# Decoder block on one core: first two units interleaved, silu and sigmoid by tanh, units and selectors in another order, last norm in three steps

## The chip, the cores and the metric

The kernel runs on 1 core of one Trainium2 chip. The metric is the device time of one execution in microseconds (us). The engines are called as in the profile: PE (matmuls; PEld is its weight loading), ACT (activations, casts and copies), DVE (elementwise work on two operands), POOL (here only DMA issues that accumulate, and memsets) and SP (DMA issues). L188 is line 188 of the kernel before.

## The reference

One decoder block on x (512 tokens, 1024 channels), with 16 learned meta tokens ahead of it. All is in float32.

```python
xn = rmsnorm(h, norm1_g)
(mq, mk, mv, mi, mf, mo, gq, gk, gv, ga, gr, gate_m, gate_g) = split(xn @ w_in)
mq, mk = silu(causal_conv(concat(mq, mk)))            # 4 taps per channel
logi, logf = mi + b_i, log_sigmoid(mf + b_f)
hm = mlstm(mq, mk, mv, logi, logf)                    # 4 heads, exp gates, running max
y_m = head_rmsnorm(hm) * sigmoid(mo)
loga = log_sigmoid(ga @ g_a2 + b) / 16
y_g = head_rmsnorm(gla(gq, gk, gv, loga)) * silu(gr)  # 4 heads
h = h + (sigmoid(gate_m) * (y_m @ w_branch_m) + sigmoid(gate_g) * (y_g @ w_branch_g)) @ w_out
h = h + (silu(hn @ w_ff_gate) * (hn @ w_ff_up)) @ w_ff_down     # hn = rmsnorm(h, norm2_g)
out = rmsnorm(h, final_g)                             # meta tokens dropped
```

## The kernel before, in words

Everything is kept transposed, channels on the partitions and tokens along the row: 528 tokens (16 meta, 512 real). Precision is kept by parts: a float32 operand is split into a high part (`hi`, a cast on ACT) and a low part (`lo`, the rest, a subtraction on DVE), and a product is three matmuls, hi*hi, hi*lo and lo*hi (`mm3`, L302 to L304).

The work of PE is a list of units (`job_list`, L51). A unit is 128 output channels against all 1024 inputs; its weights are one 128x1024 tile, loaded by SP (`load_raw`, L181), cast by ACT (`whi`, L188) and subtracted by DVE (`wlo`, L193), some units ahead (`begin`). A unit over all 528 tokens is 8 x 2 x 3 matmuls of 264 columns in two PSUM banks (`unit_all`), one over the 512 real tokens 8 x 3 of 512 in one bank (`unit_real`). From the unit gm0 on, many units go in pairs (`pair`, L350 on): seven products of half size in place of eight (L344 to L346), whose sums are put together by ACT copies (L404, L405, L407) and DVE rows.

The order of the units is: gates, then for each mLSTM head h mq, mk, two mv, two mo; then the pairs gm (gates of the branch) with the GLA units gq/gk, gv, gr; then bm, gg, bg, out, and the feed-forward fg, fu, down. The order of all instructions on each engine is written by the program itself: side work (conv, gate rows, mLSTM heads, normalised x) is held in generators, and after each step of a unit `tick` lets each of them issue a little; the numbers after `yield` are ticks to stand by. All engines run their queue in order. There are eight PSUM banks, used in turn (`bank`), so a matmul that starts a bank waits for whoever reads that bank's earlier contents.

The start: SP loads parameters, the first weights and x, eight tiles x0 to x7. ACT and DVE split weights and x times norm1_g (L471), ACT squares x, DVE adds the squares up (L482). PE runs the unit gates, then the unit mq0, both on x that is not yet divided by its norm, and then the matmul with ones (L1078), which sums the squares over channels. `rsqrt_mean` (L489) makes rstd of it: Ln and Exp on ACT and one Newton step on DVE (L496 to L500). Later evacuations multiply by rstd (L593, L615), until `normed_x` (L508, L517) has made divided x.

For the mLSTM, `conv` (L707, L716) puts four taps on ACT and DVE, `conv_act` applies silu on ACT and splits q and k (L730, L732). `gate_rows` (L633 on) makes the log gates, cumulated along the tokens, on 32 partitions; PE transposes their copies (L699) into one bank, which DVE copies to `acol` (L693). Each head (`mlstm`, L868) needs `acol`, casts its selector `sel` on ACT (L872), waits six ticks, spreads gate rows over partitions by two matmuls (L875, L876) in two banks, reads them (L879 copy on ACT, L880 on DVE, `em` by Exp on ACT), and then multiplies exps with q-k products (L897 to L899, L904) and values (L939 to L941).

[...] `act` (L130 to L132) gives the function its set: Exp and Ln one set, Silu one, Sigmoid one; a row ACT_TABLE_LOAD stands where the set changes.

At the end `final` (L1482 to L1495) makes the last norm for the second half of the tokens: Ln and Exp on ACT, four rows on DVE (L1488 to L1491), four products with the output tiles and their DMAs.

## Time and profile before

| | |
|---|---|
| three timed runs, median | 948.4 us |
| three timed runs, lowest and highest | 947.27 and 948.83 us |
| the profiled execution, its own time | 948.52 us |
| its span, first to last instruction | 946.7 us |
| mean granted clock of TensorE | 0.992 |
| PE busy, first and last matmul | 917.5 us, 6.56 and 937.5 us |
| DVE, ACT busy | 636.2, 546.2 us |
| ACT_TABLE_LOAD | 35 rows of 1.28 us |

A row of a timeline gives the start, the length, the engine, line and operation, the tiles written and read, their shapes, a count, and in brackets how long the engine idled before it and which engine, tile and line released it. A row of a window gives for PE, PEld, DVE, ACT and POOL the busy time and the number of instructions, and then the granted clock, the DMA share and GB/s. Matmuls overlap: two that follow each other start closer than either is long.

### The profile page before, as it was taken

The numbers are of one execution on the slowest core, as the hardware profiler recorded it, in microseconds if no ns is written. First come the engines' busy times: TensorE is split into PE (matmuls) and PEld (weight loads), VectorE is DVE, ScalarE is ACT, GpSimd is POOL, SyncE is SP. The second block draws the span as 40 slices with busy tenths as digits, with TensorE's granted clock in tenths as the row PEclk, the third lists the DMA queues.
The fourth block names the chain that finished last, engine by engine and source line by source line (L and its number), as shares of the span: only waits on it lengthen the run. The fifth ranks groups of instructions, "written<-read, shape, count | busy, mean of one in ns | idle before, by whom it ended". The sixth has DMA issues, their size and how long they took to land.

```text
span 946.7 us, 15478 instructions
## 1 busy us (share of the span) xinstructions
PE 917.5 (97%) x6083; PEld 842.3 (89%) x6083; DVE 636.2 (67%) x940; ACT 546.2 (58%) x954; POOL 86.8 (9%) x102
## 2 busy tenths in 40 slices
PE   6999999989999999999999999999999999999995
PEld 6988899878998899999998888888999999888885
DVE  6797776767875577777777556785767767842323
ACT  7557788779684256766874334443555555732321
POOL 0000022001100011110100000212121110000000
PEclk9999999989999999999999999999999999999998
DMA  7245375345562466655643343335788885322302
GB/s 262 101 139 155 119 162 123 75 112 134 127 163 90 111 148 155 163 120 141 134 134 107 116 133 116 107 102 132 185 186 179 189 191 148 115 94 85 111 1 89
DMA packets 48712, 124.45 MB, mean 131 GB/s; under 512 B 5376, under 2 KB 11520, under 8 KB 48640
## 3 DMA queue, kind: packets, MB, share of 16 engines
q1 hardware_dynamic: 35008, 101.32, 34.5%
q0 software_dynamic: 12544, 21.11, 14.5%
q8 instruction: 47, 0.77, 0.3%
q10 hardware_dynamic: 1088, 1.05, 0.3%
q14 instruction: 25, 0.20, 0.1%
HBM read 118.08 MB, written 5.37 MB: 130 GB/s over the span
## 4 chain that ended last, share of the span: by engine, by line
PE 78%; ACT 9%; DVE 8%; issue 3%; DMA 1%; DVEq 0%; SPq 0%; ACTq 0%
PE b L303 13%; PE b L302 13%; PE b L304 13%; PE b L344 12%; PE b L345 11%; PE b L346 11%; ACT t L132 4%; ACT whi L188 2%; DVE wlo L193 1%; ACT L130 1%; PE b L1056 1%; DVE t L716 1%; PE b L1058 1%; PE b L1035 1%; ACT L132 1%
## 5 line engine op out<-in xcount | busy, mean ns | idle before, releaser
L303 PE MATMUL b<-t,whi 128*128 128x512 f32 (+2 forms) x822 | 289.9, 353 | 1.0 <-DVE t L471 0.7
L302 PE MATMUL b<-t,whi 128*128 128x512 f32 (+2 forms) x774 | 274.0, 354 | 6.7 <-ACT t L132 6.6
L304 PE MATMUL b<-t,wlo 128*128 128x512 f32 (+2 forms) x774 | 270.8, 350 | 0.0
L344 PE MATMUL b<-t,whi 128*128 128x256 f32 (+1 forms) x864 | 250.0, 289 | 7.7 <-ACT t L404 6.1
L346 PE MATMUL b<-t,wlo 128*128 128x256 f32 (+1 forms) x864 | 245.1, 284 | 0.0
L345 PE MATMUL b<-t,whi 128*128 128x256 f32 (+1 forms) x864 | 245.0, 284 | 0.0
L193 DVE TENSOR_TENSOR wlo<-raw,whi 128x1024 fp32r<-128x1024 f32 x155 | 193.1, 1249 | 50.8 <-ACT whi L188 50.5
L188 ACT CAST whi<-raw 128x1024 fp32r<-128x1024 f32 x155 | 161.7, 1047 | 64.5 <-PE b L345 27.4
L303 PEld LDWEIGHTS b<-t,whi 128*128 128x128 f32 x822 | 155.8, 190 | 23.3 <-DVE t L843 1.1
L344 PEld LDWEIGHTS b<-t,whi 128*128 128x128 f32 x864 | 164.3, 190 | 9.9 <-ACT t L404 7.2
L302 PEld LDWEIGHTS b<-t,whi 128*128 128x128 f32 x774 | 147.0, 190 | 26.5 <-ACT t L132 6.6
L345 PEld LDWEIGHTS b<-t,whi 128*128 128x128 f32 x864 | 164.3, 190 | 0.5
L304 PEld LDWEIGHTS b<-t,wlo 128*128 128x128 f32 x774 | 146.8, 190 | 19.9 <-DVE wlo L193 0.3
L346 PEld LDWEIGHTS b<-t,wlo 128*128 128x128 f32 x864 | 164.0, 190 | 0.0
L132 ACT ACTIVATE t<-t 128x512 f32<-128x512 f32 (+6 forms) x124 | 70.4, 588 | 29.8 <-DVE t L1289 9.3
L183 POOL DMA_DIRECT2D raw<-wst x36 | 31.2, 867 | 364.4 <-DMA wf<-wst 104.9
L188 ACT CAST whi<-wf 128x1024 fp32r<-128x1024 f32 x36 | 37.8, 1051 | 22.5 <-PE b L345 13.5
L132 ACT ACTIVATE t<-f 128x256 f32<-128x256 f32 (+1 forms) x24 | 11.6, 482 | 61.6 <-DVE f L1456 61.6
L212 POOL DMA_DIRECT2D wf<-wst x36 | 32.5, 912 | 155.3 <-DMA wf<-wst 85.7
L193 DVE TENSOR_TENSOR wlo<-wf,whi 128x1024 fp32r<-128x1024 f32 x36 | 43.9, 1218 | 0.0
L1456 DVE TENSOR_TENSOR f<-f,b 128x512 f32<-128x512 f32 (+1 forms) x9 | 5.7, 629 | 53.3 <-PE b L304 53.3
L344 PE MATMUL b<-t,wgh 128*128 128x256 f32 (+1 forms) x144 | 41.0, 285 | 0.0
(219 smaller groups left out, 1216.6 us busy)
## 6 DMA issues: line engine op xcount, KB each, us to landing
raw<-wst SPq DMA_DIRECT2D x155, 512.0 KB, 3.6
wf<-wst SPq DMA_DIRECT2D x36, 256.0 KB, 3.2
wf<-wst POOLq DMA_DIRECT2D x36, 256.0 KB, 5.4
raw<-wst POOLq DMA_DIRECT2D x36, 256.0 KB, 4.7
t<-xT SPq DMA_DIRECT2D x8, 264.0 KB, 5.6
pos<-t SPq DMA_DIRECT2D x8, 264.0 KB, 2.3
t<-xT SPq DMA_DIRECT2D x8, 256.0 KB, 3.8
t<-neg POOLq DMA_DIRECT2D x6, 272.0 KB, 6.3
```

The costliest lines, as they stand in the source:

```text
L130: S.preload_act_table_set(want)
L132: S.activation(o, i, func, **kw)
L183: G.dma_start(lr(r, 0), lr(wst[v - 1], 0), accum_op=ALU.add)
L188: S.copy(t, src)
L193: V.tensor_tensor(t, src, hi.bitcast(F32), ALU.subtract)
L212: G.dma_start(lr(st.f, 1), lr(wst[u + 1], 1), accum_op=ALU.add)
L302: T.matmul(o, w_h, ah[:, c0:c1], start=first, stop=False)
L303: T.matmul(o, w_h, al[:, c0:c1], start=False, stop=False)
L304: T.matmul(o, w_l, ah[:, c0:c1], start=False, stop=last)
L344: T.matmul(o, h, xh_[k][:, c0:c1], start=start and k == 0, stop=False, skip_group_check=not start)
L345: T.matmul(o, h, xl_[k][:, c0:c1], start=False, stop=False, skip_group_check=not start)
L346: T.matmul(o, l, xh_[k][:, c0:c1], start=False, stop=k == 3, skip_group_check=not start)
```

## The change

- **First two units side by side.** `first_units` runs gates and mq0 together, for each of the eight parts of x first the six matmuls of the one, then the six of the other. Their weights are loaded, cast and subtracted in halves, between the loads and splits of x0 to x4. Ten matmuls of a constant tile with itself are issued ahead of them. The additions of the squares have one weight subtraction (unit 2) among them.
- **Tables.** Sigmoid becomes tanh of half the argument, with the plus one put into the product that follows (`branch`, the head's output) and the half into a later factor (`halfg`, the split of the branch sum). Silu of q and k becomes tanh, one more DVE row (L778 of the changed kernel) and a half in the split (L783, L786). Exp and tanh are asked from one set, `exp_and_others`; Exp keeps the set that is there if it has it. Silu of gr and of the feed-forward stays.
- **Order of the units.** The two mo of a head come after mq and mk of the next.
- **Gate rows.** The unit gates is copied from its banks by ACT right after the first units, and multiplied by rstd in one DVE row.
- **Selectors.** The first is cast at the end of `gate_rows`' row part, each next one right after the two matmuls of the head before; the six ticks go.
- **Weights** are split one unit less far ahead of time up to the fifth unit, and from there in a later place of the unit (`LATE`) until the distance is made up.
- **Last norm.** (sum + n eps)(-0.5/n) is made from the bank beside Ln and Exp, and the Newton step after them has two rows and the final product in one: three in place of four. The last output DMA goes out on SP, not on ACT.

```diff
-TABLE = {AF.Exp: LOGEXP, AF.Ln: LOGEXP, AF.Silu: "silu", AF.Sigmoid: "sigmoid"}
+TABLE = {AF.Exp: (LOGEXP, TANHEXP), AF.Ln: (LOGEXP,), AF.Tanh: (TANHEXP,), AF.Silu: ("silu",)}
...
-        o += one(("mq", h), ("mk", h), ("mv", 2 * h), ("mv", 2 * h + 1), ("mo", 2 * h), ("mo", 2 * h + 1))
+        o += one(("mq", h), ("mk", h)) + (mo(h - 1) if h else []) + one(("mv", 2 * h), ("mv", 2 * h + 1))
+    o += mo(H - 1)
...
-        if want is not None and want != table[0]:
-            if want == LOGEXP:
-                S.preload_act_table_set(want)
-            table[0] = want
+        if want is not None and table[0] not in want:
+            table[0] = want[0]
+            if func != AF.Silu:
+                S.preload_act_table_set(want[0])
...
+    LATE = {"s": [(split_hi, 4), (split_lo, 6)]}
...
         if all(i[0] == "s" for i in ITEMS[n - 2:n + 1]) and len(names) == 1 and more:
             n += 1
+            if u > 4 and ready[0] < min(n, len(ITEMS)) - 1:
+                tables = [PLAIN, LATE]
...
+    for _ in range(10):
+        T.matmul(idle[:, :P], ones, ones, start=True, stop=True)
...
-        gsb = tt()
-        for a in range(2):
-            c = slice(a * HALF, (a + 1) * HALF)
-            V.tensor_tensor(gsb[:96, c], ps[0][a][:96], rstd[:96, c], ALU.mult)
+        V.tensor_tensor(gsb[:96], gsb[:96], rstd[:96], ALU.mult)
...
         for b, a in ((q, src[0].v), (k, src[1].v)):
-            act(a, a, AF.Silu)
+            t = tt(n=a.shape[1])
+            act(t, a, AF.Tanh, scale=0.5)
+            V.scalar_tensor_tensor(a, t, 1.0, a, ALU.add, ALU.mult)
...
-            S.copy(hi, a)
+            act(hi, a, AF.Copy, scale=0.5)
             yield 2
-            V.tensor_tensor(lo, a, hi.bitcast(F32), ALU.subtract)
+            V.scalar_tensor_tensor(lo, a, 0.5, hi.bitcast(F32), ALU.mult, ALU.subtract)
...
+    def selector(h):
+        gts.sel = mpool.tile([P, 2, P], F32R, tag="sel", name=nm("sel"), bufs=1)
+        S.copy(gts.sel, cn[:, NS + h:NS + 8:H].unsqueeze(2).to_broadcast([P, 2, P]))
...
-    ps_g = unit_all(("gates", 0))
-    ps_q = unit_all(("mq", 0))[0]
+        for k in range(KT):
+            for o, ws in zip(ps, w):
+                for a in range(2):
+                    mm3(o[a], ws, k, X.h[k], X.l[k], a * HALF, (a + 1) * HALF, k == 0, k == KT - 1)
...
-        V.tensor_tensor(t, ps, t, ALU.mult)
+        V.scalar_tensor_tensor(t, t, 1.0, ps, ALU.add, ALU.mult)
...
         act(y, ps, AF.Ln, bias=b_eps, scale=1.0 / D)
+        V.tensor_scalar(x, ps, D * EPS, -0.5 / D, op0=ALU.add, op1=ALU.mult)
         act(y, y, AF.Exp, scale=-0.5)
         yield 1
         V.tensor_tensor(t, y, y, ALU.mult)
-        V.scalar_tensor_tensor(t, ps, D * EPS, t, ALU.add, ALU.mult)
-        V.tensor_scalar(t, t, -0.5 / D, 1.5, op0=ALU.mult, op1=ALU.add)
-        V.tensor_tensor(y, y, t, ALU.mult)
+        V.tensor_tensor(t, t, x, ALU.mult)
+        V.scalar_tensor_tensor(y, t, 1.5, y, ALU.add, ALU.mult)
```

Three places of the order that the program writes. The first is DVE's queue around the copy of the gate columns (`acol`). Before, the copy stands behind the first conv row (L716) of head 1's q:

```order
L508 SCALAR_TENSOR_TENSOR t_137_767<-t_5_79,pr_69,t_64_317 128x528
L707 MEMSET t_138_769 128x3
L593 TENSOR_TENSOR t_138_769<-b_122_669,t_64_317 128x264
L593 TENSOR_TENSOR t_138_769<-b_123_670,t_64_317 128x264
L716 SCALAR_TENSOR_TENSOR t_139_779<-t_138_769,pr_69,t_139_779 128x512
L693 COPY acol_574<-b_132_714 128x480
```

The same place in the changed program, where L767 is the conv row, L778 the plus one of tanh, L786 the low part of q or k, L561 and L570 rows of the normalised x, and L197 a low part of weights:

```order
L767 SCALAR_TENSOR_TENSOR t_134_770<-t_133_763,pr_71,t_134_770 128x528 x3
L197 TENSOR_TENSOR wlo_140_799<-raw_101_581,whi_135_776 128x1024
L570 TENSOR_TENSOR t_137_779<-t_132_761,t_136_778 128x528
L778 SCALAR_TENSOR_TENSOR t_122_698<-t_141_817,t_122_698 128x512
L778 SCALAR_TENSOR_TENSOR t_134_770<-t_142_821,t_134_770 128x528
L561 SCALAR_TENSOR_TENSOR t_147_837<-t_6_83,pr_71,t_64_335 128x528
L786 SCALAR_TENSOR_TENSOR t_144_829<-t_122_698,t_143_828 128x512
L744 COPY acol_604<-b_139_789 128x480
L786 SCALAR_TENSOR_TENSOR t_149_844<-t_134_770,t_148_843 128x528
```

The copy (L744) now has the convs of head 1's q and k, their tanh rows and the split of q ahead of it.

The second is PE's queue. Before, the spread of the gate rows for head 0 (L875, L876) stands inside the unit mv2 (banks 152 and 153):

```order
L304 MATMUL b_153_850<-t_15_122,wlo_121_657 128x264
L875 MATMUL b_157_866<-t_96_545,sel_144_799 128x512
L876 MATMUL b_158_867<-t_96_545,sel_144_799 128x512
L302 MATMUL b_152_849<-t_17_126,whi_115_638 128x264
L303 MATMUL b_152_849<-t_18_128,whi_115_638 128x264
```

In the changed program it is in the unit mo1, 22 rows before mv2 begins (banks 171 and 172); these rows are that beginning:

```order
L820 MATMUL b_170_911<-pr_71,t_92_505 128x128
L820 MATMUL b_170_911<-pr_71,t_102_590 128x128
L309 MATMUL b_171_916<-t_16_134,whi_123_707 128x264
L310 MATMUL b_171_916<-t_19_140,whi_123_707 128x264
L311 MATMUL b_171_916<-t_16_134,wlo_129_734 128x264
L309 MATMUL b_172_917<-t_16_134,whi_123_707 128x264
```

By the turn of the banks, 171 is the bank of the gate columns (139, read by `acol`'s copy), 172 the one of em (155).

The third is ACT's queue ahead of the first copy of the pair gm0 (L404 before), which also holds the sigmoid of mo6 and mo7 (L132 out of a bank) and the rows of head 3:

```order
L132 ACT_TABLE_LOAD
L132 ACTIVATE t_2302<-b_2122 128x512
L132 ACTIVATE t_2303<-b_2206 128x512
L879 COPY t_2329<-b_2319 128x512
L188 CAST whi_2338<-raw_2123 128x1024
L130 ACT_TABLE_LOAD
L132 ACTIVATE t_2331<-b_2320,cb 128x512
L404 COPY t_2293<-b_2289 128x256
```

In the changed program the copy is L411, tanh stands for sigmoid, and L973 is a cast of head 3's weights `wh`:

```order
L135 ACT_TABLE_LOAD
L136 ACTIVATE t_444_2420<-b_400_2232 128x512
L136 ACTIVATE t_445_2421<-b_422_2324 128x512
L973 CAST wh_394_2198<-t_431_2377 128x16
L990 CAST t_448_2446<-t_397_2204 128x512
L192 CAST whi_450_2452<-raw_401_2233 128x1024
L411 COPY t_442_2411<-b_438_2407 128x256
```

The load between the sigmoids and em is gone from here, and head 3's work stands further along at this point.

## The prediction

> **What bounds the kernel now.** I read the page first, then the waits of PE by stretch, then the windows, then the timelines of single places. The page says that PE is the engine that counts:

> ```profile
> span 946.7 us, 15478 instructions
> PE 917.5 (97%) x6083; PEld 842.3 (89%) x6083; DVE 636.2 (67%) x940; ACT 546.2 (58%) x954; POOL 86.8 (9%) x102
> ```

> The profiled execution took 948.52 us, 1.8 more than its span and 0.1 more than the median of 948.4. With PE at 97%, the change can gain only what PE waits, what it runs at a lower clock, and the ends. The waits of PE from 71.2 to 280 us, and before that:

> ```profile
> PE b L344 <- ACT t L404: 5.6, 3, 3.6
> PE b L939 <- DVE t L757: 1.6, 1, 1.6
> PE b L344 <- ACT t L405: 1.1, 1, 1.1
> PE b L748 <- ACT t L591: 0.5, 1, 0.5
> PE b L302 <- DVE t L757: 0.2, 1, 0.2
> ...
> PE b L875 <- ACT sel L872: 1.9, 1, 1.9
> ```

> The columns are total, times and longest. The five rows of 71 to 280 us sum to 9.0 us, and 3.6 of it is one wait. It has a second price, which the windows show:

> ```profile
> 195.73 0.39 PE L899 MATMUL b<-t,t 128*128 128x512 f32 x1
> 199.71 0.58 PE L344 MATMUL b<-t,whi 128*128 128x256 f32 x1 [3.59 <-ACT t L404]
> ...
> 198.40:205.20 6.80, 5.49 (x24) 0.50 0.62 152
> ```

> In a window row the length, PE's busy time and then the granted clock stand: 0.50 for 6.8 us. PE worked from 199.71 to 205.2, 5.5 us, at half speed: 2.7 us lost at most; against the spacing of the same matmuls elsewhere I find 2.3, and take 2.5. The wait at 67.44 was shorter, and left the clock alone:

> ```profile
> 67.44 0.28 PE L304 MATMUL b<-t,wlo 128*128 128x264 f32 x1
> 69.60 0.50 PE L875 MATMUL b<-t,sel 128*128 128x512 f32 x1 [1.87 <-ACT sel L872]
> ...
> 60.00:80.00 20.00, 18.00 (x139) 17.24 (x138) 18.48 (x30) 14.01 (x25) 0.00 (x0) 1.00 0.54 178
> ```

> So a wait of 2 us costs itself, one of 3.6 costs about 6. The window also shows DVE (its third pair) busy for 18.48 of 20 us just there: in this stretch DVE has nothing to spare, though its mean over the span is 67%.

> **The change part by part.** *First units.* The sum of squares (L1078) starts as soon as PE has ended two units:

> ```profile
> 22.23 1.06 PE L1078 MATMUL b<-t,ones 128*128 128x264 f32 x4
> ...
> 13.67 1.44 DVE L471 SCALAR_TENSOR_TENSOR t<-t,pr,t 128x528 fp32r<-128x528 f32 x2
> 15.02 5.59 DVE L482 TENSOR_TENSOR t<-t,t 128x528 f32<-128x528 f32 x7
> 20.53 3.49 DVE L193 TENSOR_TENSOR wlo<-raw,whi 128x1024 fp32r<-128x1024 f32 x3
> 24.52 0.71 DVE L496 TENSOR_TENSOR t<-t 128x528 f32<-128x528 f32 x1 [0.50 <-ACT t L132]
> ```

> DVE's sum was ready at 20.6, PE came at 22.23. Now PE can start on half a tile of weights instead of a whole one, which I put at 2 us earlier for all of its 96 matmuls, 20.2, and more if the ten dummy matmuls bring the clock up early. Then DVE's sum is last, or as late: seven additions 5.59 plus one subtraction now placed among them (3.49/3, 1.2) is 6.8, and they start at 13.4 to 14.0, for x arrives as before (the halves move the same bytes on the same queue). That gives 20.2 to 20.8; I take 20.3, 1.9 earlier. An idle PE of 1 to 2 us ahead of it should leave the clock, by the wait at 67.44; the bound is 2.5 lost. L496 came 2.29 after the start of L1078, so its successor (L549) starts at 22.6.

> *DVE between there and the gate columns.* The new order of units puts mq1 and mk1 ahead of mo0 and mo1, and the tanh form of silu puts one more row on DVE for each q and k. All this is ahead of the copy of the gate columns (acol), which now follows both convs. Durations of what comes in addition:

> ```profile
> L193 DVE TENSOR_TENSOR wlo<-raw,whi 128x1024 fp32r<-128x1024 f32 x6 | 7.3, 1209 | 0.0
> L593 DVE TENSOR_TENSOR t<-b,t 128x264 f32<-128x264 f32 x10 | 3.8, 423 | 0.1
> L716 DVE SCALAR_TENSOR_TENSOR t<-t,pr,t 128x512 f32<-128x512 f32 x5 | 3.7, 749 | 1.2 <-ACT t L132 1.1
> L615 DVE TENSOR_TENSOR t<-b,t 128x512 f32<-128x512 f32 x2 | 1.3, 670 | 0.0
> L732 DVE TENSOR_TENSOR t<-t,t 128x512 fp32r<-128x512 f32 x1 | 0.7, 691 | 0.0
> ...
> 43.36 0.70 DVE L649 TENSOR_TENSOR t<-t,t 32x528 f32<-32x528 f32 x1 [3.13 <-ACT t L132]
> ...
> 68.15 0.65 DVE L693 COPY acol<-b 128x480 f32<-128x480 f32 x1
> 68.72 1.53 DVE L716 SCALAR_TENSOR_TENSOR t<-t,pr,t 128x512 f32<-128x512 f32 x2
> ```

> Counted in the order of both programs, from L496 to acol: one subtraction more (1.2), five rows of conv more (3.8), the four new tanh rows, which have L716's form (3.0), a third split of q and k, all three in the dearer form (0.9), two evacuations more (0.8); two L615 fewer (-1.3), one gate row for two (-0.1). That is 8.3; rows overlap by up to 0.08 (acol ends at 68.80, the next starts at 68.72), so I take 7.7. Before, the way from 24.52 to 68.80 took 44.3, waits included (3.13 of them for Ln at 43.36). I keep the waits: the new tanh rows wait for ACT too, but ACT drops two table loads there, and the sign is open, +-3. acol then ends at 22.6 + 44.3 + 7.7 = 74.6, against 68.8.

> *Who waits for that.* In the changed program mv2's first matmul takes the PSUM bank that acol's copy empties, its second bank that of the exponentials em on ACT. ACT reaches em from the second split of k, which waits for the tanh row of DVE that ends 2.1 ahead of acol. From there it has seven rows:

> ```profile
> L188 ACT CAST whi<-raw 128x1024 fp32r<-128x1024 f32 x155 | 161.7, 1047 | 64.5 <-PE b L345 27.4
> L132 ACT ACTIVATE t<-t 128x512 f32<-128x512 f32 (+6 forms) x124 | 70.4, 588 | 29.8 <-DVE t L1289 9.3
> ```

> one cast of weights (1.05) and six of the size of the second row or half of it (3.1): 4.1, less 2.1, so em is 2.0 behind acol, at 76.6. PE itself, by before's 71.1 for the same amount of matmuls, less the wait of 2.0 and the 1.9 gained, would be there at 67.2, or 71 where lower parts of mk1 and mo0 come late; both waits lie under the later one. So PE goes on at 76.6: 5.5 behind before's row:

> ```profile
> 71.15 0.29 PE L304 MATMUL b<-t,wlo 128*128 128x264 f32 x1
> ```

> Its last wait, 5 to 6 us, is longer than the 3.59 that halved the clock, so 2.5 more; nothing to 3.4 as bounds.

> *Later waits, and ACT.* One set now serves tanh and exp, and the changed program holds 26 table loads where the one before holds 35, these 34 and one first:

> ```profile
> L130 ACT ACT_TABLE_LOAD x17 | 21.8, 1283 | 0.3
> L132 ACT ACT_TABLE_LOAD x17 | 21.8, 1283 | 0.3
> ...
> 193.59 1.28 ACT L132 ACT_TABLE_LOAD   x1
> 194.89 1.09 ACT L132 ACTIVATE t<-b 128x512 f32<-128x512 f32 x2
> 197.41 1.28 ACT L130 ACT_TABLE_LOAD   x1
> 199.29 0.36 ACT L404 COPY t<-b 128x256 f32<-128x256 f32 x1
> ...
> 179.37 0.65 ACT L591 COPY t<-b 128x264 f32<-128x264 f32 x2
> ```

> By the rows that is 9 x 1.28 = 11.5 us of ACT, and none of PE unless ACT is what PE waits for. [...] From 77 to gm0 DVE and ACT have room, as a window of that stretch shows (third and fourth pair):

> ```profile
> 120.00:140.00 20.00, 20.00 (x132) 18.20 (x130) 15.36 (x29) 16.25 (x34) 4.86 (x4) 1.00 0.73 162
> ```

> The selector is cast a head earlier, and the waits at L939, L748 and L302 should go. At gm0 the wait need not: the product q6 adds into the bank of q1, and waits for ACT's copy s1 of it (L404), which stood 20.3 us behind the evacuation at 179.37. In the new order the same two ends hold 43 rows with still two loads (2.6) and four casts of weights (4.2); by the durations of the same forms in this trace they sum to 20.5. The exps of the last head have come in where two waits were. So I let the 3.6 and its 2.5 of clock stand, as they stood. Of the other 5.4 of waits I let 0.5 stand: gain 4.9, with 0 as the other bound, since half of them lie behind gm0, where ACT is fullest.

> *Small ones.* Branch products turn from TENSOR_TENSOR to the STT form, +0.06 each, off the path while PE is ahead. The last output goes out on SP instead of ACT: I take that as nothing, with the length of the row below as the bound either way. In the tail one row leaves the chain:

> ```profile
> 939.84 0.29 DVE L1490 TENSOR_SCALAR t<-t 128x256 f32<-128x256 f32 x1
> ```

> It goes beside Ln, -0.3.

> **The sum** against the profiled 948.52: +5.5 (mv2) +2.5 (clock there) -4.9 (later waits) -0.3 (tail) = +2.8, 951.3. The gain of 1.9 at the start is inside the 5.5.

> **Rivals.** *1. ACT is in time at gm0* and the clock stays full: PE's lag from mv2 has let ACT run ahead, or the rows of the last head are done before 179. It decides once 3.6 of ACT's 20.5 us are done earlier. For it speaks that by the program 11 loads stand ahead of that copy where 18 stood, 9 us less; against it that the two inside stay. -3.6 -2.5: 945.2, faster.

> *2. DVE is earlier at acol.* The Ln wait of 3.13 goes, since silu's load no longer stands before it. acol at 71.5, PE resumes at 73.5, the wait at mv2 is under 3 us and the clock stays: -3.1 -2.5, 945.7, faster.

> *3. The waits in the gate stage stay*, with ACT as late as its window of 220 to 240 shows it (the fourth pair):

> ```profile
> 220.00:240.00 20.00, 18.93 (x144) 18.58 (x145) 13.78 (x25) 19.01 (x36) 3.06 (x5) 1.00 0.53 130
> ```

> +4.9: 956.2, slower by more than the forecast.

> [...]

> **How the numbers follow.** A measurement here can tell 0.2%, 1.9 us, from no change: same is 946.5 to 950.3. The forecast has 0.45, with its own range of 948.3 to 954.3 from the +-3 of DVE's waits: 0.32 of it above 950.3, 0.11 same, 0.02 below. Rival 1 has 0.20 (0.16 faster, 0.04 same), rival 2 0.18 (0.13 and 0.05), rival 3 0.17, slower. Together: faster 0.31, same 0.20, slower 0.49. The range of 944.5 to 956.0 takes in both faster rivals singly and half of the third; both faster ones at once (939) and the far end of the third are left out.

> **What would show it.** Right: L1164 (the sum of squares) near 20.3; acol's copy near 74; mv2's first matmul behind a wait of 4 us or more and a half clock near 77 to 83; at gm0 a wait of 3 to 4 for the copy s1 (L411). Wrong: PE at mv2 before 73 with no halving, or no wait at gm0. Also wrong, with a result near 948, if the time comes out by the start and tail alone.

## The result and the profile after

The changed kernel takes 957.3 us in the median of four runs (956.93 to 957.45), the kernel before 948.0 in the same comparison. The ratio is 1.0098 with a 95% interval of 1.0085 to 1.0111: slower by 9.3 us. The forecast was slower by 2.8, at 951.3, with 956.0 as the end of its range. The way was right, the size was not. Executions that were disturbed are left out of all comparisons, and since the only profile of the run e12 is of such an execution (1288 us), nothing is read from it.

The head of the page and the five largest of the waits of PE over the whole span (total, times, longest):

```profile
span 955.4 us, 15518 instructions
PE 923.8 (97%) x6103; PEld 847.0 (89%) x6103; DVE 643.5 (67%) x950; ACT 538.1 (56%) x948; POOL 86.7 (9%) x102
...
PE b L351 <- ACT t L411: 8.2, 3, 6.0
PE b L309 <- DVE acol L744: 3.9, 1, 3.9
PE b L1164 <- DVE t L533: 2.4, 1, 2.4
PE b L311 <- DVE wlo L197: 2.1, 2, 1.5
PE b L309 <- ACT t L136: 1.5, 2, 0.9
```

ACT has lost 8 us of work. PE waits more than before in three places: 8.2 for the copies of the pairs (L411, before 6.1), 3.9 for acol, 2.4 for the sum of squares. The timeline of PE, and of DVE at acol:

```profile
20.98 2.01 PE L1164 MATMUL b<-t,ones 128*128 128x264 f32 x4 [2.40 <-DVE t L533]
...
24.22 0.71 DVE L549 TENSOR_TENSOR t<-t 128x528 f32<-128x528 f32 x1 [2.16 <-ACT t L136]
...
75.80 0.65 DVE L744 COPY acol<-b 128x480 f32<-128x480 f32 x1
...
76.59 0.56 PE L309 MATMUL b<-t,whi 128*128 128x264 f32 x1 [3.87 <-DVE acol L744]
78.49 0.59 PE L309 MATMUL b<-t,whi 128*128 128x264 f32 x1 [0.90 <-ACT t L136]
...
204.75 0.28 PE L353 MATMUL b<-t,wlo 128*128 128x256 f32 x1
211.03 0.58 PE L351 MATMUL b<-t,whi 128*128 128x256 f32 x1 [6.00 <-ACT t L411]
```

The first of the two waits at mv2 is for acol's bank, the second for em's, as forecast. The wait at gm0 is 6.0, not 3.6. Three windows of the granted clock (length, PE busy, then the clock):

```profile
21.20:24.50 3.30, 3.30 (x12) 2.89 (x12) 1.14 (x2) 2.10 (x4) 0.00 (x0) 0.50 0.66 248
75.80:82.50 6.70, 5.01 (x20) 4.72 (x21) 5.88 (x11) 6.54 (x16) 0.00 (x0) 0.50 0.44 144
208.90:215.60 6.70, 4.57 (x21) 4.57 (x22) 3.24 (x7) 3.00 (x6) 1.72 (x2) 0.50 0.73 122
```

Between the start and the last matmuls the clock was halved three times, each time behind a wait; in the kernel before, once.

To see where the 8.7 us of the span went I compared the times at which both kernels reach the same amount of matmul work, each matmul weighed with its usual spacing. This distance is called the lag from here on, and its place is given by the time in the profile of before. By that the changed kernel is 3.8 us ahead at the end of the first two units, 0.5 behind at 30 us, 4.5 behind from 55 to 67 (parts of weights that come late, L192 and L197), 9.4 at 72 to 100, 7.1 at 104, 6.9 at 195, 9.2 at 210 behind gm0, 6.5 at 222, 7.8 at 250, and 8.7 at the end.

### The profile page after: what moved, and what is told of

Its sections match the earlier page's. It is cut to its first block, busy times and chain, and to the rows that moved or that the text cites. A ratio compares the mean times of both kernels' runs of the same rounds, so it can differ in the third digit from the quotient of the medians.

```text
span 955.4 us, 15518 instructions
## 1 busy us (share of the span) xinstructions
PE 923.8 (97%) x6103; PEld 847.0 (89%) x6103; DVE 643.5 (67%) x950; ACT 538.1 (56%) x948; POOL 86.7 (9%) x102
## 3 DMA queue, kind: packets, MB, share of 16 engines
q10 hardware_dynamic: 1232, 1.09, 0.3%
## 4 chain that ended last, share of the span: by engine, by line
PE 85%; DVE 7%; ACT 5%; issue 2%; DMA 1%; SPq 0%; DVEq 0%; ACTq 0%
PE b L309 14%; PE b L310 14%; PE b L311 14%; PE b L351 12%; PE b L353 12%; PE b L352 12%; ACT t L136 3%; DVE wlo L197 1%; PE b L1123 1%; ACT L135 1%; DVE t L767 1%; PE b L1125 1%; PE b L1102 1%; ACT whi L192 1%; DMA t<-xT 1%
## 5 line engine op out<-in xcount | busy, mean ns | idle before, releaser
L197 DVE TENSOR_TENSOR wlo<-raw,whi 128x1024 fp32r<-128x1024 f32 x153 | 191.1, 1249 | 82.4 <-ACT whi L192 82.1
L192 ACT CAST whi<-raw 128x1024 fp32r<-128x1024 f32 x153 | 160.0, 1046 | 97.6 <-PE b L310 52.3
L136 ACT ACTIVATE t<-t 128x512 f32<-128x512 f32 (+6 forms) x139 | 80.0, 593 | 51.0 <-DVE t L1171 26.7
L192 ACT CAST whi<-wf 128x1024 fp32r<-128x1024 f32 x36 | 37.8, 1050 | 23.5 <-PE b L352 13.8
L197 DVE TENSOR_TENSOR wlo<-wf,whi 128x1024 fp32r<-128x1024 f32 x36 | 43.8, 1217 | 0.0
L351 PE MATMUL b<-t,wgh 128*128 128x256 f32 (+1 forms) x144 | 40.9, 284 | 0.0
L352 PE MATMUL b<-t,wgh 128*128 128x256 f32 (+1 forms) x144 | 40.8, 284 | 0.0
L353 PE MATMUL b<-t,wgl 128*128 128x256 f32 (+1 forms) x144 | 40.8, 283 | 0.0
```

The lines of the kernel that those rows point to most:

```text
L136: S.activation(o, i, func, **kw)
L192: S.copy(t, src)
L197: V.tensor_tensor(t, src, hi.bitcast(F32), ALU.subtract)
L351: T.matmul(o, h, xh_[k][:, c0:c1], start=start and k == 0, stop=False, skip_group_check=not start)
L352: T.matmul(o, h, xl_[k][:, c0:c1], start=False, stop=False, skip_group_check=not start)
L353: T.matmul(o, l, xh_[k][:, c0:c1], start=False, stop=k == 3, skip_group_check=not start)
```

## The experiments

Each run was compared with the kernel before anew. Its median was 947.1 to 947.4 us in these comparisons, against 948.0 in that of the result. So a difference to the changed kernel is given twice: by the medians, and by the two ratios, as parts of 947 us. The interval of a ratio reaches 0.9 to 1.7 us to either side.

**e1: the order of units alone put back.**

```diff
-        o += one(("mq", h), ("mk", h)) + (mo(h - 1) if h else []) + one(("mv", 2 * h), ("mv", 2 * h + 1))
-    o += mo(H - 1)
+        o += one(("mq", h), ("mk", h), ("mv", 2 * h), ("mv", 2 * h + 1)) + mo(h)
```

> The changed kernel with the units in the order of before (mo of a head right after its mv). Theory (the copy of the gate columns stands behind head 1's conv rows in DVE's queue, and PE waits for the PSUM banks that it and em hold): acol's copy ends near 70 instead of 76.4, PE's wait of 4.0 + 1.2 at mv2 shrinks to 2 or less and the half clock behind it goes; about 9 us faster than the changed kernel, 947 to 950. Rival (the tanh rows and the denser DVE and ACT queues are what delays, wherever the units stand): 953 to 957.

Measured 951.2 us, 1.0043 of before (1.0027 to 1.0059): less than the changed kernel by 6.1 by the medians and 5.2 by the ratios, and a little more than the theory's 947 to 950. The wait for acol is gone, but waits of 3.2 us for low parts of weights (2.1 in the changed kernel) and the wait at gm0 stay:

```profile
PE b L350 <- ACT t L410: 7.6, 3, 6.1
PE b L310 <- DVE wlo L196: 3.2, 2, 1.7
```

So the order of units does not make gm0 late.

**e2: silu of q and k in one ACT row again**, in place of tanh and the two STT forms.

```diff
-            t = tt(n=a.shape[1])
-            act(t, a, AF.Tanh, scale=0.5)
-            V.scalar_tensor_tensor(a, t, 1.0, a, ALU.add, ALU.mult)
+            act(a, a, AF.Silu)
...
-            act(hi, a, AF.Copy, scale=0.5)
+            S.copy(hi, a)
...
-            V.scalar_tensor_tensor(lo, a, 0.5, hi.bitcast(F32), ALU.mult, ALU.subtract)
+            V.tensor_tensor(lo, a, hi.bitcast(F32), ALU.subtract)
```

> The changed kernel with silu of q and k as one ACT row with its own table again, no tanh row on DVE. Theory (DVE's queue ahead of acol sets mv2): the four rows gone are 3.0 us, PE resumes at mv2 near 75.5 instead of 78.5, 954 to 955. Rival (table loads on ACT are what counts): slower than the changed kernel by the loads that come back, 958 to 961.

Measured 953.9, 1.0074 (1.0056 to 1.0092): 3.4 less by the medians, 2.3 by the ratios. That is about the size of the four tanh rows ahead of acol (3.0), as if the loads that came back cost nothing. But the path is not the one expected: PE waits for neither acol nor em here, while its clock is halved for 17 us from 54.5. The size fits better than the mechanism.

**e3: the gate transposes and acol's copy seven ticks earlier.**

```diff
-        yield 8
+        yield 3
...
-        yield 2
         V.tensor_copy(acol, pst[:, :480])
```

> The changed kernel with the gate transposes and the copy to acol issued 7 ticks earlier, so that the copy stands ahead of head 1's tanh rows. Theory (two banks hold PE, acol's and em's, and em ends at 78.4 behind ACT's other rows): the wait for acol goes, and most of its time comes back as a wait for em; 955.5 to 957.5. Rival (acol's copy alone is what holds PE): mv2 goes on near 74, the clock stays full, 949 to 952.

Measured 950.7, 1.0035 (1.0022 to 1.0049): 6.6 less by the medians, 6.0 by the ratios, where the theory gave almost nothing. acol ends at 70.6, and em on ACT goes with it, since a head begins when acol is issued:

```profile
69.92 0.65 DVE L743 COPY acol<-b 128x480 f32<-128x480 f32 x1
...
70.88 0.68 ACT L136 ACTIVATE t<-b,cb 128x512 f32<-128x512 f32 x1
...
PE b L309 <- DVE t L968: 2.5, 1, 2.5
PE b L351 <- ACT t L411: 2.5, 1, 2.5
```

The first wait is the one that came instead at mv2, for a product of the head. The second is gm0: 2.5 in place of 6.0. My picture of em as a second, independent holder fell, and the gm0 wait turned out to hang on where the heads' work stands.

**e4: the start of before**, gates and mq0 one after the other, weights whole, no dummy matmuls.

```diff
-    ps_g, ps_q = first_units()
+    ps_g = unit_all(("gates", 0))
+    ps_q = unit_all(("mq", 0))[0]
```

> The changed kernel with the start of before: gates and mq0 one after the other, weights whole, no dummy matmuls. Theory (what counts from the start to mv2 is DVE's chain from the sum of squares, which began at 24.2 in the changed kernel and at 24.5 before): within 0.8 us of the changed kernel, 956.5 to 958. Rival (PE was 3.8 us ahead of before at the end of the first two units, and that lead is worth its time): 959.5 to 961.

Measured 956.1, 1.0094 (1.0078 to 1.0110), just under the theory's 956.5 to 958: the 3.8 us that PE leads after the first units buy nothing. DVE's chain began at 24.76 here, at 24.22 with the new start.

**e5: dummy matmuls in the wait for the sum of squares.**

```diff
+    idle = bank()
+    for _ in range(12):
+        T.matmul(idle[:, :P], ones, ones, start=True, stop=True)
```

> The changed kernel with twelve dummy matmuls (constant tile by itself) in the 2.4 us that PE waits for the sum of squares, so that the clock is not halved there. Theory (DVE's chain from the sum of squares to the gate columns decides): the sums' chain gets 0.9 us shorter, its half-clock share, and the end with it: 956.0 to 956.8. Rival (PE's own work at half clock from 21 to 24.5 counts): 953.5 to 955.6.

Measured 956.5, 1.0104 (1.0089 to 1.0119): inside what the theory gave, and not apart from the changed kernel's 1.0098. No half clock stands behind the sum of squares, and others stand at 57.1 and 77.6. It tells only that the loss there is small.

**e6: dummy matmuls at gm0**, 44 in the changed kernel.

```diff
+        if names[0] == ("gm", 0):
+            hh, (xx, _) = w["q1"][0], x["q1"]
+            for _ in range(44):
+                T.matmul(by, hh[:, :P], xx[0][:, cols[0]:cols[1]], start=True, stop=True)
         seven(bx, w, x, "q6", False, hook, *cols)
```

> The changed kernel with 44 dummy matmuls of 256 columns (5.2 us) in the wait of 6.0 at gm0's product q6, written to a bank that the pair clears later. Theory (a stretch in which PE is idle over about 2 of 3.4 us halves the clock for what follows): the wait stays, the half clock of 6.8 us behind it goes: 954.2 to 955.4. Rival (the clock there falls for another reason, or the dummies come in the way): 956.8 or more.

Measured 954.9, 1.0085 (1.0068 to 1.0102). The time is within the expected 954.2 to 955.4; it is 2.4 less than the changed kernel by the medians, but only 1.2 by the ratios, whose intervals overlap, so the gain is likely and its size open. The effect on the clock is plain. The window behind the wait of the changed kernel has the clock at 0.50; here it is full:

```profile
210.00:216.00 6.00, 5.57 (x43) 1.00 0.79 146
```

**e8: the same in the kernel before**, with 24 of them.

> The kernel before with 24 dummy matmuls of 256 columns (2.9 us) in its wait of 3.6 at gm0. Theory of the clock as above: no half clock from 198.3 to 205.2: 945.0 to 946.2 where before takes 948.0 (947.1 in the last comparison; then 0.9 less). Rival: no change.

Measured 945.9, 0.9984 of before (0.9975 to 0.9994): 1.3 less by the medians and 1.5 by the ratio, where 1.8 to 3.0 was expected. The window that had 0.50 before:

```profile
198.40:205.20 6.80, 5.95 (x47) 1.00 0.63 153
```

This is one insertion that computes nothing, and is faster than the kernel before.

**e7: e1, e2 and e4 together.** What is left of the change is tanh for the gates, the selectors (cast early, without the six ticks), the gate rows, the rule for late splits and the last norm.

> The changed kernel with the units in the order of before, silu of q and k in one row, and the start of before; tanh for the gates, early selectors, gate rows, late splits and the last norm stay. Theory (order and tanh rows lengthen DVE's queue ahead of acol, the start gains nothing): PE does not wait for acol or em, nor for the selector: 945 to 948. Rival (the later pieces of the mLSTM heads make ACT late at gm0 in any case): 949 to 952.

Measured 949.5, 1.0028 (1.0017 to 1.0039): the rival. PE no longer waits for acol, and still for 6.1 us at gm0, with 1.6 ahead of it for DVE:

```profile
PE b L350 <- ACT t L410: 6.1, 1, 6.1
PE b L350 <- DVE t L919: 1.6, 1, 1.6
```

So the suspects for gm0 were the selectors, tanh, the gate rows and the late splits.

**e9: as e7, but the selectors as before.**

```diff
-        sel = gts.sel
+        sel = mpool.tile([P, 2, P], F32R, tag="sel", name=nm("sel"))
+        S.copy(sel, cn[:, NS + h:NS + 8:H].unsqueeze(2).to_broadcast([P, 2, P]))
+        yield 6
```

> As e7, but each head casts its selector when it begins and stands by six ticks, as before. Theory (the early selectors put head 3's exps and its casts that wait for DVE ahead of gm0's copy in ACT's queue): the copy has only one load of two and head 3's first rows ahead of it, the wait at gm0 falls from 6.1 to 2.3, no half clock: 943.5 to 945.5. Rival (the wait of 6 comes from tanh or the gate rows): 948.5 to 950.

Measured 942.2, 0.9949 (0.9936 to 0.9962): 7.3 less than e7 by the medians, 7.5 by the ratios, and faster than both kernels. All that PE waits from 60 to 280 us:

```profile
PE b L350 <- ACT t L410: 3.7, 2, 2.3
PE b L884 <- ACT sel L881: 2.2, 1, 2.2
...
195.84 0.39 PE L350 MATMUL b<-t,whi 128*128 128x256 f32 x1 [1.41 <-ACT t L410]
```

Of the 3.7, 1.4 is at gm0 (the third row), where the clock stays full; the other 2.3 ends at 210.21, in the gate stage. The gates' tanh and the shared table, with the gate rows, the late splits and the last norm beside them, are together a gain of 5 us on the kernel before, when order, start, silu and selectors stay. No run takes them apart.

**e10: e9 with the 24 dummy matmuls at gm0 and the last output on ACT.**

> As e9, with the 24 dummy matmuls at gm0 and the last output DMA on ACT again. Theory: the clock at gm0 is full already, so the dummies bring nothing or 0.4 less; the DMA 0.3 less: 943 to 945. Rival (the clock is still halved in e9): 2 less than e9.

Measured 943.3, 0.9958 (0.9945 to 0.9970), not apart from e9: there was no half clock left at gm0 that the dummies could spare, and the queue of the last output makes no difference (from the last matmul to the end 9.29 us in e9, 9.30 here).

**e11: the changed kernel with the selectors as before**, nothing else.

> The changed kernel with the selectors and the six ticks of before, and nothing else. Theory: gm0's wait falls from 6.0 to 2 to 4; at mv2 acol stays late, and the wait for em goes with the later matmuls of the spread: 952 to 955. Rival (the selectors do not matter in this order of units): 956.5 to 958.

Measured 950.1, 1.0028 (1.0017 to 1.0039): less than the changed kernel by 7.2 by the medians and 6.6 by the ratios, and less than the theory's 952 to 955. acol's copy is as late as in it, but the wait of PE is put down to the selector:

```profile
75.99 0.65 DVE L743 COPY acol<-b 128x480 f32<-128x480 f32 x1
...
77.61 0.50 PE L934 MATMUL b<-t,sel 128*128 128x512 f32 x1 [2.20 <-ACT sel L931]
...
PE b L351 <- ACT t L411: 2.8, 2, 2.3
```

The spread stands six ticks later, inside mv2, so mv2's first banks are others. That acol no longer matters does not follow: PE stands still from 75.41 to 77.61, and acol's copy ends inside that time, at 76.64, ahead of the selector. The third row holds no wait at gm0: its 2.3 ends at 216.24, in the gate stage.

**e13: the changed kernel with the six ticks alone put back**, the selector still cast early.

```diff
         sel = gts.sel
+        yield 6
```

> The changed kernel with the six ticks back before the spread of the gate rows, the selector still cast early: one line. Theory (the ticks taken out put em's bank and acol's bank under mv2, and head 3 ahead of gm0's copy): like e11 without its wait of 2.2 for the selector: 946.5 to 949.5. Rival (the early cast itself is what delays): 955 to 957.5.

Measured 949.0, 1.0015 (1.0005 to 1.0024): 8.4 less than the changed kernel by the medians, 7.9 by the ratios. So about 8 of the 9.3 us come from one line. ACT's queue at gm0 shows how most of it comes. Of the changed kernel, ahead of the copy L411:

```profile
205.13 0.31 ACT L973 CAST wh<-t 128x144 fp32r<-128x144 f32 x1 [0.94 <-DVE t L969]
205.35 0.37 ACT L823 CAST t<-b 128x256 fp32r<-128x256 f32 x1
205.73 1.28 ACT L135 ACT_TABLE_LOAD   x1
207.03 1.09 ACT L136 ACTIVATE t<-b 128x512 f32<-128x512 f32 x2
208.00 0.21 ACT L973 CAST wh<-t 128x16 fp32r<-128x16 f32 x1
209.14 0.62 ACT L990 CAST t<-t 128x512 fp32r<-128x512 f32 x1 [0.94 <-DVE t L986]
209.67 1.04 ACT L192 CAST whi<-raw 128x1024 fp32r<-128x1024 f32 x1
210.61 0.36 ACT L411 COPY t<-b 128x256 f32<-128x256 f32 x1
```

And of e13:

```profile
196.70 1.09 ACT L136 ACTIVATE t<-b 128x512 f32<-128x512 f32 x2
197.87 0.59 ACT L945 COPY t<-b 128x512 f32<-128x512 f32 x1
198.35 1.06 ACT L192 CAST whi<-raw 128x1024 fp32r<-128x1024 f32 x1
199.30 0.70 ACT L136 ACTIVATE t<-b,cb 128x512 f32<-128x512 f32 x1
199.88 0.37 ACT L411 COPY t<-b 128x256 f32<-128x256 f32 x1
```

PE does not wait for this copy. With the ticks, it comes when head 3 has only begun (L945, em). Without them, head 3's rows up to the last cast stand ahead of it, and two of these casts (L973, L990) wait 0.94 each for a product on DVE.

At mv2 the line changes less. PE still waits there for acol, now at the first matmul of the spread:

```profile
75.56 0.51 PE L939 MATMUL b<-t,sel 128*128 128x512 f32 x1 [2.54 <-DVE acol L744]
```

The wait of 0.9 for em behind it and the half clock are gone, the latter in line with the last section: the 2.54 lay across a boundary of the clock's grid (1.6 us before 74.6 and 1.0 behind it). By the lag, e13 is 5.9 behind the kernel before at 85 us, where the changed kernel is 9.4 to 9.7. About 0.9 of that difference is not the line's: acol's copy ends that much earlier, at 75.51, since the clock stayed full at the sum of squares (L549 begins at 23.26, not 24.22), which is long before the line acts. At gm0 the difference is larger: from 195 to 210 us e13 gains 5.9 on the kernel before, where the changed kernel loses 2.3. From there to the end e13 loses 2.3 again; in the gate stage PE waits 2.31, and the clock is halved from 214.5 on.

**e12: as e9 with the selector cast early**, the ticks kept.

> As e9 in the order of the heads' work (six ticks before the spread), but with the selector cast early, as in the changed kernel. Theory (the ticks place the heads' work, the early cast only takes a wait away): PE's wait of 2.2 for the selector and the half clock behind it go, gm0 stays as in e9: 938.0 to 940.5. Rival (the next of the head's operands is as late, and PE waits for that): 941.5 to 943.

Measured 943.3 in the median of four runs, 0.9954 (0.9941 to 0.9968): just above what the theory and the rival gave, and not apart from e9. So the 2.2 us that PE waits for the selector there brought nothing; where they went stays open. Against e7 this run differs by the six ticks alone, and it is 6.2 less by the medians. e7 did not wait for acol, so the ticks have most of their price without that wait too.

## Why the prediction was wrong

*First units: the start near 20.3.* It was 20.98. The halving of the clock, which I set aside with "2.5 lost" as its bound, came: it followed a wait of 2.4 and made the chain from the sum of squares to L549 3.24 long instead of 2.29. L549 came at 24.2, forecast 22.6.

*DVE's queue: 52.0 from L549 to the end of acol.* From 24.22 to 76.45 are 52.2. This term held to 0.2, in part because two small misses cancel: DVE's rows grew by 7.3, not 7.7, and its waits by 0.6, not 0. It is the late start, 1.6, that made acol end at 76.45 and not at 74.6.

*em 2.0 behind acol, PE goes on at 76.6.* 2.0 it was (78.43), and PE went on at 78.5. Lag at 72 to 85 us with the clock: forecast 5.5 + 2.5 = 8.0, measured 9.4 to 9.7. The 2.5 for the clock was not measured alone at mv2; at gm0 in the kernel before, where it was taken from, e8 took the half clock away and gained 1.3 to 1.5.

*Later waits, -4.9: the step that failed.* Measured from that point to the end is a gain of 0.7. Up to 195 the waits that should go went, about 2.5 us. At gm0 the prediction says "I let the 3.6 and its 2.5 of clock stand", from 43 rows of ACT of 20.5 us. The rows themselves were counted well, and counted as if they ran back to back. Between the same two ends, 187.72 and 210.97, ACT took 23.25: 20.0 of rows, and 3.2 in which it waited, 0.73 and 0.62 at the copies of x and twice 0.94 at head 3's casts, for DVE. The sentence "The exps of the last head have come in where two waits were" had the fact in hand and left out that head 3's rows come with waits of their own. PE's wait became 6.0, not 3.6, and the lag at gm0 rose by 2.3. In the gate stage 2.7 came back up to 222 and 1.3 was lost again by 250; another 0.9 has run up slowly by the end, and I have no cause for it.

*Rival 1* (ACT in time at gm0) counted table loads ahead of the copy, seven fewer, 9 us. They are gone, as counted (11 in place of 18), and ACT was later all the same: what decided was which rows stand ahead of the copy, not how much ACT had to do. In e9, where those rows stay away, the copy is in time for the clock to stay full, which is what rival 1 had in mind. *Rival 2* gave DVE's queue a gain from Ln's wait; it was 2.93 in place of 3.13. *Rival 3* (the later waits stay, 956.2) is nearest to the result; its place was wrong, since gm0 grew and the gate stage shrank.

*The small ones.* The last norm's chain is one row shorter (from the last matmul to its first product of outputs 3.07 where it was 3.39), but from that matmul to the end of the span it is 9.52 where it was 9.49. The 0.3 did not reach the end there; in e9 and e10 0.2 of it did.

*What was not asked.* The prediction has a sentence on the selector, "cast a head earlier", as a gain. It has none on the six ticks that were taken out with it, and these are about 8 us, shown by e13, and about 6 between e7 and e12. Their going drew head 3's work ahead of gm0's copy, which is the larger part. It also put the spread's two banks just ahead of mv2; but a late acol stops PE with the ticks as well (2.54 in e13), so how much of the loss at mv2 is the ticks' stays open.

## What to carry to other kernels

In a program that orders each queue itself, a number of ticks to stand by is a placement: when it goes, look what the moved work now stands ahead of, on every engine, and whose buffers follow it in the ring. A stretch of a queue costs its rows and the waits inside it; rows that alternate with another engine can each bring a wait, and a sum of durations leaves these out (ahead of gm0, 20.0 us of rows and 3.2 of waits). When a change of many parts is slower, take its parts alone: here the tables for the gates and what came with them were worth 5 us, and one line cost about 8.

## What the runs showed of the hardware

In these runs the clock did not follow the length of a wait alone. While matmuls ran, half-clock stretches lasted 3.41 us (in the changed kernel, from 21.1), 6.83 (there from 75.75 and 208.87, and in the kernel before from 198.3) and 17 (in e2, from 54.5), near whole multiples of 3.41. Those of the changed kernel begin 16 and 39 such steps apart, on one grid. The halving went with how much PE was idle inside one step of the grid. The wait for the selector shows it. In the kernel before, 1.87 us long, it lay across a boundary, and both steps kept PE busy for 2.4 us or more:

```profile
65.20:68.60 3.40, 2.52 (x21) 1.00 0.56 216
68.60:72.00 3.40, 2.40 (x17) 1.00 0.45 104
```

In e9 the same wait, 2.15 us long, lay nearly all within one step, and the next one ran at half:

```profile
67.80:71.10 3.30, 1.29 (x8) 1.00 0.24 59
71.20:74.60 3.40, 3.40 (x16) 0.50 0.51 171
74.60:78.00 3.40, 3.40 (x29) 1.00 0.15 58
```

So the prediction's reading, that a wait of 2 us costs itself alone, held only for where that wait lay against the boundary; in e9 a wait of 2.15 was followed by half clock. And with matmuls on nothing put into the wait at gm0 the clock behind it was 1.00 in place of 0.50: in e6 (44 of them, from 210.0) and in e8 (24, from 198.4).
